# First head's weights as contiguous rows, constants joined to x's first tile, and constant products on TensorE ahead of the first weights

## The chip, the cores and the metric

The kernel runs on one core of a Trainium2 chip. The metric is the device time of one execution in microseconds (us). Before the change it is 1331.93 us, the median of three runs (1330.86, 1331.93 and 1333.83). In the profile, PE is TensorE, PEld its weight loads, DVE is VectorE, ACT is ScalarE, POOL is GpSimd, and SP is the engine that issues most DMAs.

## What is computed

One layer of a streaming encoder on x (512 tokens by 2048 channels, float32), cut to what matters:

```python
hn = rmsnorm(x, norm_g)                       # 512 x 2048
proj = einsum('bsd,dc->bsc', hn, w_in)        # q, k, v, gate of 3 branches; 4 forget logits; merge gates
f_logit = proj[..., QKVG_COLS:QKVG_COLS + N_HEADS] + b_f
gates = sigmoid(proj[..., QKVG_COLS + N_HEADS:] + b_gate)   # 3 x 2048
ya, yb, yc = forgetting(...), chunked(...), stick_breaking(...)   # 4 heads of 128 each
ys = stack([ya, yb, yc]) * silu(gate_paths)
merged = sum(gates * einsum('bsnw,nwd->bsnd', ys, w_up), axis=2)
out = x + merged @ w_out
```

## The kernel before, in words

**Layout.** Everything is held transposed: channels on the 128 partitions, the 512 tokens along the row. x is 16 tiles of 128x512 (kt 0 to 15). Each float32 operand of a product is split into a rounded part (`hi`, type fp32r) and the rest (`lo`), and hi·hi + hi·lo + lo·hi is summed: ScalarE rounds (L243, or L426 for x, where norm_g is multiplied in), VectorE subtracts (L247, or L429 for x). The row norm is not applied to x but to the products afterwards, by the tile `rstd` (L497, used at L505). Most projections use a seven-product scheme over pairs of column blocks (`PairTask`), where some weight sums are made by a DMA that adds on landing (`add_up`, L282, issued by POOL).

**Units.** The work on TensorE is a list of units, each with one tile of weights: a load (`load_unit`, L370, into one of six `raw` tiles), a rounding (`prep`, L384, into one of three `wh`/`wl` pairs), and its products (all at L262). The first nine units (`first_quad`, L1165) are the first head: q, k, v and gate at once, in a sweep over the 16 tiles of x in the order of `spans` (L413): kt 0, then kt 1, then (8, 9), (2, 3), (10, 11) and so on. A unit of one kt has 12 products of 512 columns: four of weight hi with x hi, four of weight hi with x lo, four of weight lo with x hi. A unit of two kts has 24. Between them stand the forget logits (L1213). After the sweep come two gate columns (`gate_units(late=True)`, L1154) and the rest of the heads.

**What orders the work.** A planner (`Flow`, L63) keeps a clock for PE, ACT and DVE, with costs and due times that the tasks name (`due` in `prep_x` L422, `DUE` in `combos` L510, `landing` L267 for DMAs), and writes the order of these three engines out. Each engine then runs its list in order and waits by semaphore. DMAs of SP stand in program order (`fetch`, L275); every eighth reuses a semaphore and waits for the DMA eight before it. The tiles `t2` (21 of them, `NT`) hold x, the loads of `xn` (x again, token by token, for the row norms, L466) and, later, results; one of them is `rstd`.

**The start.** ACT issues the load of the constants `small_in` (L293: norm_g, b_f, b_gate and others, 133 numbers a partition), then that of the first unit's weights. SP issues x kt 0, x kt 1, the second unit's weights, x kt 8, x kt 9, the third unit's weights, and so on. The first head's weights are cut out of the array `w_col` by a four-piece access (`src`, L1240): 128 numbers (512 bytes) a piece for the first two units, 256 (1 KB) for the others. `prep_x` rounds x kt 0 on ACT, then DVE subtracts; `prep` rounds the first weights on ACT, then DVE subtracts.

Of the kernel before, what the change touches and what calls it, by code (L numbers as in the profile page):

```python
# [15 lines left out]
P = 128  # L16
# [46 lines left out]
class Flow:  # L63
# [16 lines left out]
    def give(self, slots, n=1):  # L80
        slots.free += [self.fin] * n
# [80 lines left out]
def hybrid_kernel(  # L162
# [1 line left out]
    tc: tile.TileContext,  # L164
    xT: bass.AP,
    xn: bass.AP,
    consts: bass.AP,
    w_col: bass.AP,
    rel: bass.AP,
    w_up: bass.AP,  # L170
# [26 lines left out]
    def t2(s, dt=F32):  # L197
        return tp.tile([P, S], dt, tag="t2", name=nm(s))
# [19 lines left out]
    def two(ap):  # L218

        return ap.rearrange("p (h s) -> p h s", h=2)  # L220
# [19 lines left out]
    def split(hi, lo, src, n, ev=None, due=(), hi_ev=None):  # L240

        yield (ACT, act_us(n), *due)
        nc.scalar.activation(hi, src, AF.Copy)  # L243
        if hi_ev is not None:
            set_(hi_ev)
        yield (DVE, dve_us(n), *due)
        nc.vector.tensor_sub(lo, src, f(hi))  # L247
        if ev is not None:
            set_(ev)
# [17 lines left out]
    def landing(ready, kb):  # L267

        line[0] = max(line[0], ready) + 0.5
        line[1] = max(line[1], line[0] + 1.0) + kb / (325.0 if line[1] < 60.0 else 370.0)  # L270
        return line[1] + 1.5

    first = []

    def fetch(to, src, ready, kb, queue=nc.sync):  # L275
        i = queue.dma_start(to, src)
# [93 lines left out]
    def load_unit(u):  # L370
        if isinstance(u, Pair):
            if u is u.task.units[0]:
                yield from u.task.load()
            return
        for s in u.srcs:
            yield raws, 1
            t = raw_tile(u.shape)
            to = t
            if len(s.shape) > len(t.shape):
                to = t.rearrange("p (c k) m -> p c k m", c=s.shape[1])  # L380
            u.raw = t
            u.there.t = fetch(to, s, flow.ready, 4 * u.shape[0] * P * P // 1024, nc.scalar if u is units[0] else nc.sync).t

    def prep(u):  # L384
        n = u.shape[0] * P
        u.hi = wp.tile([P] + u.shape, F32R, tag="wh", name=nm("wh"), bufs=LA + 1)
        u.lo = wp.tile([P] + u.shape, F32R, tag="wl", name=nm("wl"), bufs=LA + 1)
        yield u.source_there()
        yield from split(u.hi, u.lo, u.source(), n, u.ready, hi_ev=u.ready_hi)
        u.split_done()  # L390


# [17 lines left out]
    del xps.free[UK:]  # L410


    spans = [(0, 1), (1, 2)] + [(k + h, k + h + 2) for k in range(0, UK, 2) for h in (0, UK)][1:]  # L413
    place = {kt: i for i, kt in enumerate(kt for sp in spans for kt in range(*sp))}


# [2 lines left out]

    def prep_x(kt):  # L420

        due = (5.0 + 2.7 * place[kt],)  # L422
        yield x_in[kt]
        x, g, h, lo = xraw[kt], gn[:, kt:kt + 1], xs[kt].hi, xs[kt].lo
        yield (ACT, act_us(S), *due)
        nc.scalar.activation(h, two(x), AF.Copy, scale=g)  # L426
        set_(raw_hi[kt])
        yield (DVE, dve_us(S), *due)
        nc.vector.scalar_tensor_tensor(lo, two(x), g, f(h), op0=ALU.mult, op1=ALU.subtract)  # L429
        set_(raw_ev[kt])  # L430

        due = (DUE[0] - 16.0 + place[kt],)
        if kt % 2 == 0:
            yield (DVE, 0.5, *due)
            nc.vector.tensor_scalar_mul(x, x, g)
# [28 lines left out]
    n_used = [0]  # L464

    def square_x(i, x):  # L466
        yield n_in[i]
# [7 lines left out]
    def norm_x():  # L475

        m, tmp = small_n[:, 2, :], [small_n[:, i, :] for i in range(3, 6)]
        yield DVE, 0.2
        nc.vector.tensor_reduce(m, ssq, axis=AX.X, op=ALU.add)
        yield from rsqrt(rcol, m, D, tmp, 4)  # L480
        yield DVE, 0.1
        nc.vector.tensor_scalar_mul(rcol_s, rcol, SCALE)
        yield t2s, 1
        dg = t2("dg")
        for b in range(QB):
            yield ACT, 0.3
            nc.scalar.activation(dg[:, blk(b)], identf, AF.Copy, scale=rcol[:, b:b + 1])
        yield Event(flow.fin + 3.0)
        yield atts, 1
        ps = att()  # L490
        yield PE, 0.9
        nc.tensor.matmul(ps, onef, dg, start=True, stop=True)
        give(t2s, 2)
        yield t2s, 1
        yield ACT, act_us(S)
        rstd.append(t2("rstd"))
        nc.scalar.activation(rstd[0], ps, AF.Copy)  # L497
        give(atts)
        set_(rstd_ev)

    def by_norm(c, src=None):

        yield rstd_ev
        yield DVE, dve_us(S)
        nc.vector.tensor_mul(c, c if src is None else src, rstd[0][:c.shape[0], :])  # L505
        n_used[0] += 1
        if n_used[0] == NB * DT + NB * NH + NH + 4 * NH + 1:
            give(t2s)

    def combos(k):  # L510

        due = (DUE[0] + 0.5 * k,)
        late = (DUE[1] + 0.5 * k,)
        yield gained[k]
        yield gained[k + UK]
        yield used_f[k // 2]
        a, b = xraw[k], xraw[k + UK]
        q = dve_us(HS)
        yield (DVE, q, *due)
        nc.vector.tensor_sub(a[:, LH], a[:, LH], a[:, RH])  # L520
# [15 lines left out]
        give(t2s)  # L536
# [627 lines left out]

    def first_quad(head):  # L1165

        c0 = head.n * 4 * NH + head.h
        ps, pools = {}, {Q: accs[1], K: accs[2], V: atts, G: atts}
        def mms(i):
            def go(u):  # L1170
# [66 lines left out]
            return  # L1237
            yield

        def src(k0, k1):  # L1240
            half, k0, k1 = k0 // UK, k0 % UK, (k1 - 1) % UK + 1
            return w_col[c0:c0 + 3 * NH + 1:NH, half, :, k0:k1, :].rearrange("c p k m -> p c k m")
        return [Unit(mms(i), after if sp[1] == KT else None, shape=(4 * (sp[1] - sp[0]), P), srcs=[src(*sp)])
                for i, sp in enumerate(spans)]

    def schedule(head, a, b):
# [243 lines left out]

    def loads():
        def x(kt):
            yield t2s, 1
            xraw[kt] = t2("x")
            x_in[kt].t = fetch(xraw[kt], xT[kt], 0.0, 256).t

        def n(i):
            yield t2s, 1
            t = t2("xn")
            n_in[i].t = fetch(t, xn[i // NQ, i % NQ], 0.0, 256).t  # L1500
            spawn(square_x(i, t), 10.0)

        todo = list(range(NQ * QB))
        for i, sp in enumerate(spans):

# [35 lines left out]
    assert not side, side  # L1541


NT = 21
KEPT = 1
NX = 28
# [48 lines left out]
```

## Time and profile before

| what | us |
|---|---|
| median of three runs | 1331.93 |
| the profiled execution, whole | 1331.46 |
| its span, first to last instruction | 1329.7 |
| PE busy in the span | 1317.4 |
| DVE busy | 1134.5 |
| ACT busy | 806.3 |

A row of the timeline reads: start, duration of the merged instructions, engine, line, operation, out<-in, how many; then in brackets the engine's idle time ahead of it and what ended it. A row of the windows reads: stretch, its length, busy time of PE, PEld, DVE, ACT and POOL with the count of instructions, the granted clock of TensorE, the share of the DMA engines, GB/s. A row of the waits reads: engine and line <- who released it: us in total, times, the longest. A row of the chain reads: start, us, what.

### The profile page before, as it was taken

To read this page: it belongs to the slowest core of one execution; us is meant where nothing else is said; L and a number is where in the kernel's file an instruction comes from. 1 tells how busy PE (TensorE), PEld (TensorE's weight loads), DVE (VectorE), ACT (ScalarE), POOL (GpSimd) and SP (SyncE) were. 2 spreads that over 40 slices of the span, in tenths; PEclk is the share of its full clock that TensorE was granted. 3 is DMA by queue.
4 is the path that set the end of the run, shared out by engine and by line. 5 is a ranking of instruction groups with operands and counts; after the bars stand their busy time and mean duration, and the time that the engine had idled before them with its cause. 6 is when DMAs were issued, how large, how long until landed. Compare 5 with 4: busy or idle time off the path is not lost.

```text
span 1329.7 us, 20204 instructions
## 1 busy us (share of the span) xinstructions
PE 1317.4 (99%) x7490; PEld 1149.0 (86%) x7490; DVE 1134.5 (85%) x1675; ACT 806.3 (61%) x1280; POOL 94.8 (7%) x120
## 2 busy tenths in 40 slices
PE   8999999999999999999999999999999999999998
PEld 5888888888888888888888888888888888888887
DVE  7899888788888889888988979888899877897786
ACT  8777557575566665666556665666557655454443
POOL 0000000010000100000010100001000000000100
PEclk9999999999999999999999999999999999999999
DMA  9876677767776777767777677676768856668883
GB/s 312 230 188 171 187 201 188 199 171 200 195 209 165 205 204 184 212 158 210 202 182 205 163 207 200 188 202 175 198 179 273 276 193 193 186 173 241 238 238 108
DMA packets 93251, 266.24 MB, mean 200 GB/s; under 512 B 10576, under 2 KB 17360, under 8 KB 93152
## 3 DMA queue, kind: packets, MB, share of 16 engines
q1 hardware_dynamic: 73472, 203.79, 45.6%
q0 software_dynamic: 15552, 56.63, 24.9%
q10 hardware_dynamic: 4128, 4.53, 1.0%
q8 instruction: 59, 0.97, 0.3%
q14 instruction: 40, 0.33, 0.1%
HBM read 245.21 MB, written 19.70 MB: 199 GB/s over the span
## 4 chain that ended last, share of the span: by engine, by line
PE 98%; DVE 1%; DMA 0%; issue 0%; ACT 0%; DVEq 0%
PE acc L262 84%; PE att L262 8%; PE att L998 1%; PE att L257 1%; PE att L258 1%; PE att L1111 1%; PE att L1112 1%; PE att L259 1%; PE att L1110 1%; DVE wl L247 0%; PE att L1062 0%; DMA raw<-in_w_col 0%; PE att L1213 0%; PE att L899 0%; PE att L900 0%; DVE m L247 0%
## 5 line engine op out<-in xcount | busy, mean ns | idle before, releaser
L247 DVE TENSOR_TENSOR wl<-raw,wh 128x1024 fp32r<-128x1024 f32 (+2 forms) x419 | 500.7, 1198 | 145.0 <-ACT wh L243 137.7
L243 ACT ACTIVATE wh<-raw 128x1024 fp32r<-128x1024 f32 (+2 forms) x419 | 434.7, 1038 | 149.3 <-PE acc L262 61.9
L262 PE MATMUL acc<-x,wh 128*128 128x512 f32 (+1 forms) x1568 | 399.4, 391 | 6.8 <-ACT wh L243 6.8
L262 PEld LDWEIGHTS acc<-x,wh 128*128 128x128 f32 x1568 | 277.6, 190 | 55.8 <-ACT wh L243 7.2
L262 PE MATMUL acc<-t,wh 128*128 128x512 f32 (+1 forms) x1128 | 283.8, 390 | 0.0
L262 PEld LDWEIGHTS acc<-t,wh 128*128 128x128 f32 x1128 | 198.3, 189 | 32.8
L262 PEld LDWEIGHTS acc<-x,wl 128*128 128x128 f32 x1504 | 207.0, 190 | 18.0 <-DVE wl L247 1.7
L262 PE MATMUL acc<-x,wl 128*128 128x256 f32 (+1 forms) x1504 | 217.0, 285 | 0.6 <-DVE wl L247 0.6
L262 PEld LDWEIGHTS acc<-t,wl 128*128 128x128 f32 x1104 | 151.7, 190 | 11.4
L262 PE MATMUL acc<-t,wl 128*128 128x256 f32 x1104 | 155.5, 283 | 0.0
L282 POOL DMA_DIRECT2D raw<-in_w_col x92 | 79.5, 864 | 926.7 <-DMA raw<-in_w_col 529.7
L262 PE MATMUL acc<-m,wh 128*128 128x512 f32 (+1 forms) x512 | 113.7, 366 | 1.5 <-DVE m L247 1.5
L262 PEld LDWEIGHTS acc<-m,wh 128*128 128x128 f32 x512 | 85.5, 190 | 14.4 <-DVE m L247 1.9
L805 ACT ACTIVATE c<-acc 128x256 f32<-128x256 f32 x51 | 19.5, 383 | 97.2 <-PE acc L262 94.2
L772 ACT ACTIVATE u<-acc 128x512 f32<-128x512 f32 x51 | 30.3, 594 | 79.4 <-PE acc L262 79.4
L751 ACT ACTIVATE u<-acc 128x512 f32<-128x512 f32 x52 | 31.1, 598 | 72.2 <-PE acc L262 69.3
L627 DVE TENSOR_TENSOR raw<-raw,raw 128x1024 f32<-128x1024 f32 x54 | 65.9, 1220 | 0.5
L621 DVE TENSOR_TENSOR raw<-raw,raw 128x1024 f32<-128x1024 f32 x54 | 65.9, 1220 | 0.4
L262 PE MATMUL att<-y,wh 128*128 128x512 f32 x256 | 65.8, 389 | 0.0
L262 PEld LDWEIGHTS acc<-m,wl 128*128 128x128 f32 x448 | 60.6, 191 | 3.8
L262 PE MATMUL acc<-m,wl 128*128 128x256 f32 x448 | 62.5, 282 | 0.0
L262 PEld LDWEIGHTS att<-y,wh 128*128 128x128 f32 x256 | 48.1, 188 | 10.0
(191 smaller groups left out, 1389.8 us busy)
## 6 DMA issues: line engine op xcount, KB each, us to landing
raw<-in_w_col SPq DMA_DIRECT2D x237, 512.0 KB, 4.3
raw<-in_w_col POOLq DMA_DIRECT2D x92, 512.0 KB, 6.5
raw<-in_w_out SPq DMA_DIRECT2D x40, 512.0 KB, 4.0
gl<-c SPq DMA_DIRECT2D x48, 256.0 KB, 3.6
raw<-in_w_up SPq DMA_DIRECT2D x32, 384.0 KB, 3.8
sg<-gl SPq DMA_DIRECT2D x48, 256.0 KB, 5.1
raw<-in_w_out POOLq DMA_DIRECT2D x16, 512.0 KB, 6.1
x<-in_xT SPq DMA_DIRECT2D x16, 256.0 KB, 6.4
```

The costliest lines, as they stand in the source:

```text
L243: nc.scalar.activation(hi, src, AF.Copy)
L247: nc.vector.tensor_sub(lo, src, f(hi))
L257: nc.tensor.matmul(ps, lh, rh, start=start, stop=False, skip_group_check=more)
L258: nc.tensor.matmul(ps, lh, rl, start=False, stop=False, skip_group_check=more)
L259: nc.tensor.matmul(ps, ll, rh, start=False, stop=stop, skip_group_check=more)
L262: nc.tensor.matmul(ps, w, x, start=start, stop=stop, skip_group_check=more)
L282: nc.gpsimd.dma_start(to, src, accum_op=ALU.add)
L621: nc.vector.tensor_add(w[1], w[1], w[5])
L627: nc.vector.tensor_add(w[2], w[2], w[1])
L751: nc.scalar.activation(self.u, ps, AF.Copy)
L772: nc.scalar.activation(self.s, ps, AF.Copy)
L805: nc.scalar.activation(c, ps[:, RH], AF.Copy, scale=-1.0)
```

## The change

- `consts` becomes `begin`: x's kt 0 and the constants in one array of 645 numbers a partition, loaded by one DMA, the first of SP. The tile `x_begin` is kt 0; it is no longer a `t2` tile, and `rstd` is later written over it, so that `NT` goes from 21 to 20. `combos(0)` sets `begin_free` in place of giving the tile back.
- The first head's weights are laid out ahead of time as `w_one` (two arrays of 128x512) and `w_two` (seven of 128x1024), so that a partition's row is 2 KB or 4 KB in one piece. The first of them is the first DMA of ACT.
- The first unit's weights are rounded on ACT in two halves of 128x256; the first half sets `ready_hi`.
- x kt 0 is rounded by VectorE (`tensor_scalar_mul`) and not by ScalarE.
- TensorE multiplies ones (bf16 views of `onef`) 16 times into `first_ps` ahead of everything else. `first_ps` is written anew later by the logits.
- The planner's numbers change: 340 for 325 in `landing`, `due` 2.5 for 5.0, `DUE` 45, 55 for 48, 58, `line` and `flow.fin`.

```diff
+    begin_in = cp.tile([P, begin.shape[1]], F32, name="begin_in")
+    x_begin, small_in = begin_in[:, :S], begin_in[:, S:]
+    first = [tc.keep_in_program_order(nc.sync.dma_start(begin_in, begin))]
-    small_in = cp.tile([P, consts.shape[1]], F32, name="small_in")
-    nc.scalar.dma_start(small_in, consts)
...
+        if u is units[0]:
+            for h in range(2):
+                yield ACT, act_us(n // 2)
+                nc.scalar.activation(u.hi[:, 2 * h:2 * h + 2, :], u.source()[:, 2 * h:2 * h + 2, :], AF.Copy)
+                if h == 0:
+                    set_(u.ready_hi)
+            yield DVE, dve_us(n)
+            nc.vector.tensor_sub(u.lo, u.source(), f(u.hi))
+            set_(u.ready)
...
-        due = (5.0 + 2.7 * place[kt],)
+        due = (2.5 + 2.7 * place[kt],)
...
+        if kt == 0:
+            yield (DVE, 0.5, *due)
+            nc.vector.tensor_scalar_mul(h, two(x), g)
...
-    rstd, rstd_ev = [], Event()
+    rstd, rstd_ev, begin_free = [x_begin], Event(), Event()
...
-        yield t2s, 1
+        yield begin_free
         yield ACT, act_us(S)
-        rstd.append(t2("rstd"))
         nc.scalar.activation(rstd[0], ps, AF.Copy)
...
-            return w_col[c0:c0 + 3 * NH + 1:NH, half, :, k0:k1, :].rearrange("c p k m -> p c k m")
+        srcs = [w_one[i] for i in range(N_ONE)] + [w_two[i] for i in range(len(SPANS) - N_ONE)]
...
+    warm = onef.bitcast(BF16)
+    for _ in range(WARM):
+        nc.tensor.matmul(first_ps[:, :2 * P], warm[:, :P], warm, start=True, stop=True)
-    line[:] = 0.8, 3.0
-    flow.fin = 5.0
+    line[:] = 0.8, 1.9
+    flow.fin = 3.5
...
-NT = 21
+NT = 20
+WARM = 16
-DUE = 48.0, 58.0
+DUE = 45.0, 55.0
```

More of the change, by code (lines that the diff above doesn't have):

```diff
@@ L166, in hybrid_kernel @@
     xn: bass.AP,
-    consts: bass.AP,
+    begin: bass.AP,
+    w_one: bass.AP,
+    w_two: bass.AP,
     w_col: bass.AP,
@@ L269, in landing @@
         line[0] = max(line[0], ready) + 0.5
-        line[1] = max(line[1], line[0] + 1.0) + kb / (325.0 if line[1] < 60.0 else 370.0)
+        line[1] = max(line[1], line[0] + 1.0) + kb / (340.0 if line[1] < 60.0 else 370.0)
         return line[1] + 1.5
-    first = []
     def fetch(to, src, ready, kb, queue=nc.sync):
@@ L377, in load_unit @@
             t = raw_tile(u.shape)
-            to = t
-            if len(s.shape) > len(t.shape):
-                to = t.rearrange("p (c k) m -> p c k m", c=s.shape[1])
             u.raw = t
-            u.there.t = fetch(to, s, flow.ready, 4 * u.shape[0] * P * P // 1024, nc.scalar if u is units[0] else nc.sync).t
+            u.there.t = fetch(t, s, flow.ready, 4 * u.shape[0] * P * P // 1024, nc.scalar if u is units[0] else nc.sync).t
     def prep(u):
@@ L388, in prep @@
         yield u.source_there()
-        yield from split(u.hi, u.lo, u.source(), n, u.ready, hi_ev=u.ready_hi)
+        if u is units[0]:
[7 more added lines that the diff above has]
+            set_(u.ready)
+        else:
+            yield from split(u.hi, u.lo, u.source(), n, u.ready, hi_ev=u.ready_hi)
         u.split_done()
@@ L410, in hybrid_kernel @@
     del xps.free[UK:]
-    spans = [(0, 1), (1, 2)] + [(k + h, k + h + 2) for k in range(0, UK, 2) for h in (0, UK)][1:]
+    spans = SPANS
     place = {kt: i for i, kt in enumerate(kt for sp in spans for kt in range(*sp))}
@@ L420, in prep_x @@
     def prep_x(kt):
-        due = (5.0 + 2.7 * place[kt],)
+        due = (2.5 + 2.7 * place[kt],)
         yield x_in[kt]
         x, g, h, lo = xraw[kt], gn[:, kt:kt + 1], xs[kt].hi, xs[kt].lo
-        yield (ACT, act_us(S), *due)
-        nc.scalar.activation(h, two(x), AF.Copy, scale=g)
+        if kt == 0:
+            yield (DVE, 0.5, *due)
+            nc.vector.tensor_scalar_mul(h, two(x), g)
+        else:
+            yield (ACT, act_us(S), *due)
+            nc.scalar.activation(h, two(x), AF.Copy, scale=g)
         set_(raw_hi[kt])
@@ L463, in hybrid_kernel @@
     squared = [0]
-    n_used = [0]
     def square_x(i, x):
@@ L505, in by_norm @@
         nc.vector.tensor_mul(c, c if src is None else src, rstd[0][:c.shape[0], :])
-        n_used[0] += 1
-        if n_used[0] == NB * DT + NB * NH + NH + 4 * NH + 1:
-            give(t2s)
     def combos(k):
@@ L535, in combos @@
         yield from split(h, lo, a[:, RH], HS, ev, late)
-        give(t2s)
+        if k:
+            give(t2s)
+        else:
+            set_(begin_free)
         if k % 2 == 0:
@@ L1165, in first_quad @@
     def first_quad(head):
-        c0 = head.n * 4 * NH + head.h
         ps, pools = {}, {Q: accs[1], K: accs[2], V: atts, G: atts}
@@ L1238, in after @@
             yield
-        def src(k0, k1):
-            half, k0, k1 = k0 // UK, k0 % UK, (k1 - 1) % UK + 1
-            return w_col[c0:c0 + 3 * NH + 1:NH, half, :, k0:k1, :].rearrange("c p k m -> p c k m")
-        return [Unit(mms(i), after if sp[1] == KT else None, shape=(4 * (sp[1] - sp[0]), P), srcs=[src(*sp)])
+        srcs = [w_one[i] for i in range(N_ONE)] + [w_two[i] for i in range(len(SPANS) - N_ONE)]
+        return [Unit(mms(i), after if sp[1] == KT else None, shape=(4 * (sp[1] - sp[0]), P), srcs=[srcs[i]])
                 for i, sp in enumerate(spans)]
@@ L1492, in x @@
         def x(kt):
+            if kt == 0:
+                xraw[kt], x_in[kt].t = x_begin, landing(0.0, 256)
+                return
             yield t2s, 1
@@ L1541, in hybrid_kernel @@
     assert not side, side
-NT = 21
+NT = 20
 KEPT = 1
+WARM = 16
+SPANS = [(0, 1), (1, 2)] + [(k + h, k + h + 2) for k in range(0, UK, 2) for h in (0, UK)][1:]
+N_ONE = 2
 NX = 28
@@ L1571, with first @@
     rel = g["rel_bias"][0]
+    xT = g["x"][0].T.reshape(DT, P, S)
+    cols = [C * 4 * NH + r * NH for r in range(4)]
+    def first(k0, k1):
+        half, k0, k1 = k0 // UK, k0 % UK, (k1 - 1) % UK + 1
+        return w_col[cols, half, :, k0:k1, :].transpose(1, 0, 2, 3).reshape(P, -1, P)
     at = np.clip(np.arange(P)[:, None] + S - P - np.arange(S)[None, :], -128, 128) + 128
     arrays = {
-        "xT": g["x"][0].T.reshape(DT, P, S),
+        "xT": xT,
         "xn": g["x"][0].reshape(QB, P, DT // NQ, S).transpose(0, 2, 1, 3),
-        "consts": np.concatenate(consts, axis=1),
+        "begin": np.concatenate([xT[0]] + consts, axis=1),
+        "w_one": np.stack([first(*sp) for sp in SPANS[:N_ONE]]),
+        "w_two": np.stack([first(*sp) for sp in SPANS[N_ONE:]]),
         "w_col": w_col,
```

## The prediction

> **What bounds the kernel now.** I read the page first, then the windows, the waits of PE, and the timeline of the first 20 us and of the end of the sweep.
>
> The page, engines and chain:
>
> ```profile
> PE 1317.4 (99%) x7490; PEld 1149.0 (86%) x7490; DVE 1134.5 (85%) x1675; ACT 806.3 (61%) x1280; POOL 94.8 (7%) x120
> PE 98%; DVE 1%; DMA 0%; issue 0%; ACT 0%; DVEq 0%
> ```
>
> TensorE is the bound: 98% of the chain that ended last is its work. The windows, cut where something changes:
>
> ```profile
> 0.00:6.60 6.60, 0.02 (x1) 0.02 (x1) 2.71 (x12) 2.71 (x4) 1.52 (x12) 1.00 0.60 168
> 6.60:11.70 5.10, 5.10 (x12) 4.04 (x13) 3.96 (x6) 3.12 (x5) 0.00 (x0) 1.00 0.95 328
> 11.70:58.50 46.80, 46.80 (x216) 34.49 (x216) 41.36 (x88) 40.86 (x95) 2.74 (x3) 1.00 0.94 304
> 58.50:70.30 11.80, 11.00 (x90) 10.59 (x89) 11.80 (x19) 8.77 (x18) 0.00 (x0) 1.00 0.41 96
> 70.30:1326.00 1255.70, 1254.23 (x7175) 1099.79 (x7176) 1074.23 (x1552) 750.82 (x1161) 90.58 (x105) 1.00 0.71 197
> ```
>
> From 70.30 to 1326.00 PE lacks 1.47 us of being always busy, so the rest of the program follows whatever PE wins or loses before, us for us. Besides that and the last stores, PE idles at two places: 6.6 us at the start, and 0.8 us in 58.5 to 70.3, where VectorE is full (11.80 of 11.80). The waits of PE say the same of the start:
>
> ```profile
> PE acc L262 <- ACT wh L243: 6.8, 2, 6.6
> ```
>
> A second loss shows in no idle time. The chain, in pairs of products:
>
> ```profile
> 6.58 1.22 PE acc L262 x2
> 10.36 0.85 PE acc L262 x2
> 11.97 0.47 PE acc L262 x2
> ```
>
> The first twelve products of 512 columns follow each other every 0.425 us (0.85 for two), the next ones every 0.23. They are the x12 of the window 6.60:11.70. The granted clock column stands at 1.00 in that window, so here the pitch and not that column tells the clock. The slow stretch costs 12 x (0.425 - 0.23) = 2.3 us. So three sums can be won: up to 6.6 us of start, 2.3 us of slow products, 0.8 us later.
>
> **The change, part by part.** The start now:
>
> ```profile
> 0.87 0.20 POOL L306 MEMSET tmpc<- 128x128 f32 x1
> 1.26 0.45 ACTq L276 DMA_DIRECT2D raw<-in_w_col  x1
> 3.99 0.72 ACT L426 ACTIVATE x<-x,small_in 128x512 fp32r<-128x512 f32 x1 [1.90 <-DMA small_in<-in_consts]
> 4.19 0.21 DVE L332 TENSOR_SCALAR gq<-small_in 128x1 f32<-128x1 f32 x2
> 4.74 0.75 DVE L429 SCALAR_TENSOR_TENSOR x<-x,small_in,x 128x512 fp32r<-128x512 f32 x1 [0.34 <-ACT x L426]
> 5.53 0.49 DVE L435 TENSOR_SCALAR x<-x,small_in 128x512 f32<-128x512 f32 x1
> 5.90 0.63 ACT L243 ACTIVATE wh<-raw 128x512 fp32r<-128x512 f32 x1 [1.19 <-DMA raw<-in_w_col]
> 6.56 0.69 DVE L247 TENSOR_TENSOR wl<-raw,wh 128x512 fp32r<-128x512 f32 x1 [0.54 <-ACT wh L243]
> ```
>
> *Weights' arrival.* They are issued at 1.26, behind the constants, and end ACT's wait at 5.90. After the change they are ACT's first DMA (the constants' place, 0.83) and have 128 rows of 2 KB instead of 512 pieces. The windows of the start give the rate:
>
> ```profile
> 1.00:2.00 1.00, 0.00 (x0) 0.00 (x0) 0.62 (x3) 1.00 (x1) 0.89 (x6) 1.00 0.14 35
> 2.00:3.00 1.00, 0.00 (x0) 0.00 (x0) 0.39 (x3) 0.08 (x1) 0.23 (x1) 1.00 0.81 189
> 3.00:4.00 1.00, 0.00 (x0) 0.00 (x0) 0.01 (x1) 0.01 (x1) 0.00 (x0) 1.00 1.04 378
> 4.00:5.00 1.00, 0.00 (x0) 0.00 (x0) 0.66 (x5) 0.71 (x1) 0.00 (x0) 1.00 0.93 249
> 5.00:6.00 1.00, 0.00 (x0) 0.00 (x0) 0.96 (x2) 0.10 (x1) 0.00 (x0) 1.00 0.64 141
> 6.00:7.00 1.00, 0.42 (x1) 0.42 (x2) 0.46 (x2) 1.00 (x2) 0.00 (x0) 1.00 0.69 209
> 7.00:8.00 1.00, 1.00 (x3) 0.74 (x3) 0.93 (x2) 0.34 (x2) 0.00 (x0) 1.00 0.94 349
> ```
>
> By 4.0 us 602 KB have come; `begin` (330 KB) and the first weights (262 KB) are 592 KB. Some of x kt 1, queued behind `begin` on SP, is mixed in, so I take 4.45 us for the weights, between 4.0 and the 5.9 of today. `begin` (today's x kt 0 and constants, usable at 3.99) I take at 4.0.
>
> *Rounding.* Only half the weights are rounded before the first product: 0.40 us by the nearest row of that size,
>
> ```profile
> 27.20 0.40 ACT L243 ACTIVATE x<-x 128x256 fp32r<-128x256 f32 x1
> ```
>
> in place of 0.63, so 4.45 + 0.05 + 0.40 = 4.9, and 0.05 to the product (6.53 to 6.58 today): 4.95. x kt 0 goes to VectorE at about 4.2 (two small copies first) and takes 0.49 as L435 does: 4.7, in time. Then x lo (0.75) ends at 5.65, L435 at 6.1, weight lo (0.69) at 6.8; the products that need them come 4 and 8 products later, at 5.9 and 6.8 even at the fast pitch. ACT loses one rounding of x (0.72), which VectorE takes over at 0.49; VectorE was idle then. Nothing of this reaches PE.
>
> *The constants.* `onef` is written by 1.07; 16 products of 256 columns follow. Their slow pitch is not in the trace: below the 0.425 of 512 columns, above half of it (0.21). Fast, sixteen of 256 columns take 2.08,
>
> ```profile
> 61.37 2.08 PE L262 MATMUL acc<-x,wh 128*128 128x256 f32 x16
> ```
>
> 0.13 each against 0.23, so I take the same part of 0.425, 0.24: 3.9 us, ending at 5.0 (bounds 4.5 and 7.9). So the first real product starts at 5.0 instead of 6.58: **1.6 us**.
>
> *The clock.* Today the pitch turns fast 5.1 us after the first product. From 1.1 us the same gives 6.2, so products between 5.0 and 6.2 are still slow: a loss of 1.2 x (1 - 0.23/0.425) = 0.55 us instead of 2.3, **1.75 us** won. Bounds: nothing lost (2.3 won), or the constants do not count and all 2.3 are lost again. The Trainium skill (TensorE: Matmul & The Clock Gate, Part 1: The HAM clock gate) says that the clock is raised after a busy window of about 3.4 us, and that these windows run freely and do not start with the kernel; the trace's 5.1 us, more than one window and less than two, agrees. By that rule an estimate for the turn here is anywhere from 4.5 to 7.9, with a gain from 1.0 to 2.3 in place of the 1.75; rival 1 prices the late end from rows.
>
> *The third unit.* 1.6 + 1.75 = 3.35 us earlier PE asks for the third unit's weights, which are late enough today to be the next wait:
>
> ```profile
> 12.34 1.06 ACT L243 ACTIVATE wh<-raw 128x1024 fp32r<-128x1024 f32 x1 [1.90 <-DMA raw<-in_w_col]
> 14.57 0.61 PE L262 MATMUL acc<-x,wh 128*128 128x512 f32 x2
> ```
>
> PE will want them at 14.57 - 3.35 = 11.2, so they must land by 10.1. From 4 to 8 us only 948 KB moved (249, 141, 209, 349), in the stretch where the 512-byte pieces are under way. At 375 they take 2.5 us: landing at 12.34 - 1.5 = 10.8 at the latest reckoning. With the whole rest (2.16 MB up to this unit, less 602 KB) at 375 after 4.0 and 0.4 for the signal it is 8.6. The middle, 9.7, costs nothing; 10.8 costs 0.7. From the fourth unit on the weights are rounded long before PE wants them:
>
> ```profile
> 16.99 1.04 ACT L243 ACTIVATE wh<-raw 128x1024 fp32r<-128x1024 f32 x1
> 21.24 0.62 PE L262 MATMUL acc<-x,wh 128*128 128x512 f32 x2
> 38.40 1.06 ACT L243 ACTIVATE wh<-raw 128x1024 fp32r<-128x1024 f32 x1 [0.67 <-PE att L262]
> ```
>
> Rounded at 18.03, wanted at 21.24; at 38.40 ACT itself waits for PE to give back a `wh`. So ACT, and behind it the `xn` loads on SP and the weights that follow them in SP's queue, move with PE.
>
> *The end of the sweep.* Here a planner's list decides, and the changed order differs:
>
> ```profile
> 49.40 1.27 ACT L487 ACTIVATE dg<-identf,small_n 128x128 f32<-128x128 f32 x4
> 54.84 1.02 PE L492 MATMUL att<-dg,tmpc 128*128 128x512 f32 x2
> 56.33 2.01 ACT L243 ACTIVATE wh<-raw 128x1024 fp32r<-128x1024 f32 x2 [1.66 <-DMA raw<-in_w_col]
> 57.42 2.36 DVE L247 TENSOR_TENSOR wl<-raw,wh 128x1024 fp32r<-128x1024 f32 x2 [1.96 <-ACT wh L243]
> 59.70 0.69 DVE L505 TENSOR_TENSOR f<-att,rstd 128x512 f32<-128x512 f32 x1
> 68.98 2.35 DVE L247 TENSOR_TENSOR wl<-raw,wh 128x1024 fp32r<-128x1024 f32 x2
> 70.26 1.22 PE L262 MATMUL acc<-x,wl 128*128 128x256 f32 x8 [0.62 <-DVE wl L247]
> ```
>
> ACT waits until 56.33 for the adding DMA's sum; from 57.42 to 70.2 VectorE works without a break and PE waits 0.62 for it (0.18 before, for ACT). After the change the norm's product (L492) stands eight products earlier, `rstd` and the product f stand ahead of the wait, in the 1.96 us that VectorE idles, and the combination c1 (0.41) behind the late `wl`. So VectorE's run from the sum to that `wl` is 0.69 + 0.41 = 1.1 us shorter, and the 0.8 us can go. Against that: ACT has one more `xn` square and one split less ahead of its 38.40 (0.4 us), so the sum may gain some 0.4 us less than PE. I take **0.4 us**, bounds 0 and 0.8. L492 stays unhurried: `dg` is done at 50.67 today, four us ahead of it, and eight products are 1.8.
>
> *Costed at nothing.* The reuse of x kt 0's tile for `rstd`, with `NT` 20: as many `t2` tiles are free for `xn` as before (21 - 1 - 16 = 20 - 1 - 15). POOL's list is the same, SP's and ACT's differ in single swaps after the first rows. PE's order after the sweep is the same instruction for instruction.
>
> **The sum.** 1.6 + 1.75 + 0.4 = 3.75 us, against the profiled execution's 1331.46: 1327.7. That execution lies 0.5 us below the median of the runs (1331.93), so for the median I say **1328.1**.
>
> **The rivals.**
> 1. *The clock turns late, or the first weights come late.* If the constants count for half, because their columns are few or because PE pauses behind them, the turn comes halfway between 6.2 and 10.1 (5.1 us after the first real product), at 8.1: a loss of 1.4 in place of 0.55. Then the third unit waits for nothing and the gain is 1.6 + 0.9 + 0 to 0.4, 1329.0 to 1329.4. If the first weights land at 5.4 and not 4.45, another 1.0 goes: 1330.4. For it: the constants last 3.9 us, less than the 5.1 that the turn takes today. Against: by 4.0 us the DMAs have moved enough for `begin` and these weights.
> 2. *The change does not do what it says*: constants do not raise the clock at all. Then the gain is 1.6 + 0.4, 1329.9, within the first rival's times.
> 3. *The sum at the first gate column does not move.* If POOL's adding DMA still lands at 56.3, VectorE's run ends 1.1 us earlier at best, and 3.35 us won become an idle PE at 69: the gain is 1.1, 1330.8. The same place gives the slow side: the kernel gets slower from the point where that DMA lands more than 1.1 us later than now, at 57.4; crowded behind loads that now come in a burst it could land at 60, 2.6 us past the point: 1334.5. Against: its source is queued behind `xn` loads that move with PE.
> 4. *All of it goes well*: 1.6 + 2.3 + 0.8 = 4.7, 1327.2; with weights at 4.0 and constants at 4.5, 1326.7.
>
> **How the numbers follow.** Forecast with its own spread (1327.3 to 1329.2) 0.55; rivals 1 (0.17) and 2 (0.05) together 0.22; rival 3 0.08 without loss and 0.06 as a loss; rival 4 0.09. The range leaves out the loss and the ends of the rest: 1326.2 to 1331.2. About 0.2% (2.7 us) is what a measurement of this kernel can tell from no change; that is 1329.3. Faster by more: the forecast, rival 4 and a little of the first: 0.66. Slower by more: most of rival 3's loss, 0.05. Within: 0.29.
>
> **What would show it.** Right: the first product with `wh` at 5.0; the pitch 0.23 from about 6; the third unit's products at 11.2 without idle time; no idle PE between 55 and 67; the rest the same. Wrong: products at 0.425 beyond 8 us; ACT waiting for `raw` of the third unit past 10.1; PE idle behind `wl` at the first gate column.

## The result, and the profile after

The changed kernel takes 1328.58 us (median of five runs, 1326.86 to 1329.00) against 1332.21 for the kernel before beside it (five runs, 1330.86 to 1333.83). The ratio is 0.9964, 95% interval 0.9953 to 0.9975: faster by 0.36%. The profiled execution went from 1331.46 to 1328.65, so by 2.81 us, and its span from 1329.7 to 1326.9. By the medians the gain is 3.63 us; the profiled execution of before lay 0.75 under its median. The changed kernel's five runs stand in two groups, 1326.9 and 1327.0 against 1328.6 to 1329.0; the experiments come back to that.

The page's engines and the waits of PE after the change:

```profile
PE 1320.2 (99%) x7506; PEld 1150.5 (87%) x7506; DVE 1134.7 (86%) x1676; ACT 805.9 (61%) x1280; POOL 94.9 (7%) x120
```

```profile
PE acc L264 <- DVE m L249: 1.5, 2, 1.3
PE att L1544 <- POOL tmpc L307: 1.1, 1, 1.1
PE acc L264 <- DVE gq L333: 0.7, 1, 0.7
```

PE is as full as before. The 6.6 us of waiting at the start have become 1.1 ahead of the constants and 0.7 behind them. The first row, 1.5 us near 1183, is the same in both kernels. The waits at the first gate column are gone.

The timeline of the start (start, us, engine, line, operation; idle time and releaser in brackets), and then the chain (start, us, what):

```profile
0.83 0.39 ACTq L276 DMA_DIRECT2D raw<-in_w_one  x1
...
1.13 3.60 PE L1544 MATMUL att<-tmpc 128*128 128x256 bf16 x16 [1.13 <-POOL tmpc L307]
...
4.61 0.17 DVE L331 COPY gq<-begin_in 128x4 f32<-128x4 f32 x1 [2.04 <-DMA begin_in<-in_begin]
...
4.79 0.72 ACT L390 ACTIVATE wh<-raw 128x256 fp32r<-128x256 f32 x2 [2.71 <-DMA raw<-in_w_one]
4.79 0.48 DVE L435 TENSOR_SCALAR x<-begin_in 128x512 fp32r<-128x512 f32 x1
...
5.42 1.19 PE L264 MATMUL acc<-x,wh 128*128 128x512 f32 x2 [0.69 <-DVE gq L333]
```

```profile
5.42 1.19 PE acc L264 x2
...
9.17 0.85 PE acc L264 x2
10.02 0.48 PE att L264 x2
10.51 0.46 PE acc L264 x2
```

The constants run from 1.13 to 4.73, 0.225 us each. `begin` ends VectorE's wait at 4.61, the weights end ScalarE's at 4.79, and the first product starts at 5.42. In the chain two products still take 0.85 us at 9.17, and about 0.47 from 10 on: in this execution the clock turns near 10, sixteen constants or not.

The loads, by the windows of the start (stretch, length, busy time of PE, PEld, DVE, ACT, POOL, granted clock, DMA share, GB/s):

```profile
4.00:5.00 1.00, 0.72 (x4) 0.18 (x2) 0.39 (x3) 0.21 (x1) 0.00 (x0) 1.00 1.11 396
5.00:6.00 1.00, 0.58 (x2) 0.52 (x3) 1.00 (x4) 1.00 (x3) 0.00 (x0) 1.00 1.00 383
6.00:7.00 1.00, 1.00 (x4) 0.81 (x3) 0.96 (x3) 0.23 (x1) 0.00 (x0) 1.00 1.07 412
7.00:8.00 1.00, 1.00 (x4) 0.81 (x3) 1.00 (x3) 0.95 (x2) 0.00 (x0) 1.00 1.02 418
```

Where the pieces of 512 bytes and 1 KB moved 141 to 349 GB/s, whole rows move 383 to 418. The third unit's weights are rounded with no wait ahead of them, and its products follow the second unit's without a gap, in the timeline:

```profile
9.66 1.06 ACT L245 ACTIVATE wh<-raw 128x1024 fp32r<-128x1024 f32 x1
```

```profile
13.09 0.62 PE L264 MATMUL acc<-x,wh 128*128 128x512 f32 x2
```

The end of the sweep, in the timeline:

```profile
52.60 0.60 ACT L507 ACTIVATE begin_in<-att 128x512 f32<-128x512 f32 x1
...
53.41 0.68 DVE L515 TENSOR_TENSOR f<-att,begin_in 128x512 f32<-128x512 f32 x1
53.78 2.01 ACT L245 ACTIVATE wh<-raw 128x1024 fp32r<-128x1024 f32 x2 [0.58 <-DMA raw<-in_w_col]
...
67.54 1.12 PE L264 MATMUL acc<-x,wl 128*128 128x256 f32 x8
68.50 1.72 PE L264 MATMUL acc<-t,wh 128*128 128x256 f32 x13
```

`rstd` is done and f is begun ahead of the adding DMA's sum, which lands at 53.78 in place of 56.33. The product behind `wl` at 67.54 has no idle time. The next row, the first product of `t`, ends the stretch. In the kernel before it stands here:

```profile
71.31 1.96 PE L262 MATMUL acc<-t,wh 128*128 128x256 f32 x15
```

PE's gate columns begin at 58.46 before and at 56.99 after, in the two timelines:

```profile
58.46 2.11 PE L262 MATMUL acc<-x,wh 128*128 128x256 f32 x16
```

```profile
56.99 2.08 PE L264 MATMUL acc<-x,wh 128*128 128x256 f32 x16
```

So this stretch took 12.85 us and now takes 11.51, which is four times the 2.88 that 24 products need. From that product on, the last product follows 1254.70 us later in both. So the 2.81 us are 1.47 won up to the end of the sweep and 1.34 won in the 12 us behind it, where the idle column had shown only 0.8.

### The profile page after: what moved, and what is told of

It reads as the page before. It is cut to its first block, busy times and chain, and to the rows that moved or that the text cites. A ratio compares the mean times of both kernels' runs of the same rounds, so it can differ in the third digit from the quotient of the medians.

```text
span 1326.9 us, 20238 instructions
## 1 busy us (share of the span) xinstructions
PE 1320.2 (99%) x7506; PEld 1150.5 (87%) x7506; DVE 1134.7 (86%) x1676; ACT 805.9 (61%) x1280; POOL 94.9 (7%) x120
## 4 chain that ended last, share of the span: by engine, by line
PE 98%; DVE 1%; DMA 0%; issue 0%; DVEq 0%
PE acc L264 84%; PE att L264 8%; PE att L1008 1%; PE att L259 1%; PE att L260 1%; PE att L1121 1%; PE att L1122 1%; PE att L261 1%; PE att L1120 1%; PE att L1072 0%; PE att L1222 0%; DMA begin_in<-in_begin 0%; PE att L909 0%; PE att L910 0%; DVE m L249 0%; DVE wl L249 0%
```

## Experiments

**Theories.** In the kernel before, three things could have cost these 2.8 us and more in the faster runs: the late start, the slow clock, and the wait at the first gate column. For the last there were two readings: the order of the planner's list there (norm ahead of the sum), or the moment at which the adding DMA's sum lands.

One table holds what the profiles say. S is where PE could begin the gate columns (the start of the first product there, less the idle time ahead of it); "landed" is the start of ACT's split of the adding DMA's sum; "ahead" is S less landed; "lost" is the time from S to the first product of `t`, less 11.51.

| execution | us | first product | clock turns | S | landed | ahead | lost |
|---|---|---|---|---|---|---|---|
| before | 1331.46 | 6.58 | 11.72 | 58.46 | 56.33 | 2.13 | 1.34 |
| after | 1328.65 | 5.42 | 9.93 | 56.99 | 53.78 | 3.21 | 0.00 |
| e1, no constants | 1329.32 | 5.80 | 10.89 | 57.64 | 53.75 | 3.89 | 0.00 |
| e2, 20 constants | 1326.75 | 5.61 | 3.82 | 55.12 | 52.06 | 3.06 | 0.00 |
| e3, norm's times alone | 1334.68 | 6.66 | 11.08 | 58.80 | 58.67 | 0.13 | 4.31 |
| e4, rows alone | 1329.08 | 5.90 | 9.84 | 57.19 | 54.02 | 3.17 | 0.30 |
| e5, old numbers | 1331.37 | 5.38 | 9.32 | 56.82 | 54.71 | 2.11 | 1.36 |
| e6, x ahead | 1326.79 | 5.39 | 4.55 | 55.14 | 52.28 | 2.86 | 0.01 |
| e7, constants alone | 1333.63 | 6.69 | 4.27 | 57.50 | 57.09 | 0.41 | 3.07 |
| e8, x by ACT | 1328.73 | 5.91 | 9.56 | 57.08 | 53.65 | 3.43 | 0.00 |
| e9, changed again | 1326.88 | 5.77 | 4.90 | 55.23 | 51.98 | 3.25 | 0.00 |
| e10, x ahead again | 1326.76 | 5.32 | 4.93 | 55.12 | 52.04 | 3.08 | 0.01 |
| e11, old norm times | 1328.66 | 5.67 | 9.68 | 57.00 | 53.35 | 3.65 | 0.00 |
| e12, old start numbers | 1332.90 | 5.60 | 10.31 | 57.41 | 56.48 | 0.93 | 2.35 |

The turns are the trace's records of the clock; the pitch of the products (0.425, then 0.23) changes at the same place. In e1 the split did not wait for the sum, so there 53.75 is the latest that it can have landed. In e3 the 4.31 hold a stretch at half the clock (see there).

### e1: no constants (changed kernel)

```diff
-WARM = 16
+WARM = 0
```

> The changed kernel without the 16 constant products; the rest of the lists is the same. Theory A (of the prediction: the constants start the count for the clock): without them the pitch turns fast 5.1 us after the first real product, and the time is 1.0 to 1.8 us above the changed kernel's, about 1330.0. Theory B (the pause of 0.7 us between the last constant and the first real product voids them, except when the turn happens to fall well): the time stays within 0.6 us of the changed kernel's 1328.6, and the turn comes 3.4 to 6.8 us after the first real product in either.

Measured: 1328.94 (11 runs, 1328.19 to 1330.68), ratio 0.9981, 0.9972 to 0.9989. Without a single constant half of the gain or more is still there (0.19% against the changed kernel's 0.36% by the ratios), and nothing is lost at the gate column. The clock turns 5.1 us after the first product, as in the kernel before. The time is theory B's and not theory A's. None of its runs is in the group at 1326.9.

### e2: twenty constants (changed kernel)

```diff
-WARM = 16
+WARM = 20
```

> 20 constant products instead of 16: at 0.225 us each they end at 5.6 in place of 4.7, so TensorE doesn't pause ahead of the first real product, which starts 0.2 us later. Theory A: no gain, within 0.3 us of the changed kernel. Theory B: the stretch from 1.1 us on is then busy throughout, the pitch turns fast between 4.5 and 8 us, and the time falls by about 1.5 us to 1327 (0.5 at least).

Measured: 1328.23 (seven runs, 1326.68 to 1328.72), ratio 0.9968, 0.9957 to 0.9978. In its profile the constants turn the clock by themselves, at 3.82, and end at 4.78, so that PE pauses 0.83 us all the same. That execution takes 1326.75: the faster group is the one with the early turn. The median is 0.35 us under the changed kernel's 1328.58: theory A allowed 0.3, theory B asked for 0.5 at least, so it decides neither.

### e3: the norm's due times alone (kernel before)

```diff
-DUE = 48.0, 58.0
+DUE = 45.0, 55.0
```

> The kernel before with DUE = 45, 55 alone. In the lists this puts rstd and f ahead of the first gate column's rounded weights on ACT and DVE; the start is as before. Theory C (the order of the lists removes the waits at the first gate column): PE idles at most 0.3 us between 58 and 70, and the time falls by 0.8 to 1.3 us, to about 1331.0. Rival D (those waits went because PE and the adding DMA stand otherwise to each other after the faster start): no change, 1332.2.

Measured: 1334.19 (11 runs, 1332.31 to 1336.26), ratio 1.0015, 1.0006 to 1.0024: slower. So an earlier norm is no gain by itself. The list of ACT moved with it, the sum landed at 58.67 in place of 56.33, and PE stood still for it. Neither theory had that. The timeline, then the windows of what follows (the third number from the end is the granted clock):

```profile
60.73 2.57 PE L262 MATMUL acc<-x,wh 128*128 128x256 f32 x16 [1.93 <-ACT wh L243]
```

```profile
58.80:62.28 3.48, 1.55 (x13) 1.55 (x14) 2.52 (x3) 3.48 (x7) 0.58 (x1) 1.00 0.92 152
62.28:65.69 3.41, 3.41 (x19) 3.41 (x18) 3.41 (x7) 2.19 (x5) 0.00 (x0) 0.50 0.42 70
```

The pause of 1.93 us was followed by 3.41 us at half the clock, where PE is full but its products of 256 columns follow each other every 0.213 us in place of 0.12.

### e4: whole rows alone (kernel before)

```diff
...
-            return w_col[c0:c0 + 3 * NH + 1:NH, half, :, k0:k1, :].rearrange("c p k m -> p c k m")
...
+        srcs = [w_one[i] for i in range(N_ONE)] + [w_two[i] for i in range(len(SPANS) - N_ONE)]
...
```

> The kernel before with w_one and w_two alone: whole rows, the constants still in a load of their own and ahead of the first weights on ACT's queue, the three lists as before. By the prediction's step on the weights: they land at about 5.0 instead of 5.9, the third unit's at 10 instead of 12.3; the first product starts at about 5.6, and the time falls by 0.9 us to 1331.3. Rival: the constants' load in front, and not the 512-byte pieces, is what holds the weights; then the first product stays at 6.3 or later and the time within 0.3 us.

Measured: 1330.92 (11 runs, 1329.08 to 1332.93), ratio 0.9990, 0.9982 to 0.9999. The profiled execution is the fastest of these. In it the sum lands 3.17 us ahead instead of 2.13, and 0.30 are lost instead of 1.34, with the old list. So the loads alone can bring most of the gain at the gate column. The first product comes at 5.90, between the 5.6 expected and the rival's 6.3. In the four windows from 4 to 8 us the DMAs moved 373, 262, 371 and 406 GB/s, against 249, 141, 209 and 349 before, so the whole rows themselves made the loads faster. Part of this execution's lead is chance: its clock turned 3.9 us after the first product, 5.1 before. What x's first tile and the constants in one load are worth alone was not run.

### e5: all four planner numbers old (changed kernel)

```diff
-        line[1] = max(line[1], line[0] + 1.0) + kb / (340.0 if line[1] < 60.0 else 370.0)
+        line[1] = max(line[1], line[0] + 1.0) + kb / (325.0 if line[1] < 60.0 else 370.0)
...
-        due = (2.5 + 2.7 * place[kt],)
+        due = (5.0 + 2.7 * place[kt],)
...
-    line[:] = 0.8, 1.9
-    flow.fin = 3.5
+    line[:] = 0.8, 3.0
+    flow.fin = 5.0
...
-DUE = 45.0, 55.0
+DUE = 48.0, 58.0
```

> The changed kernel with the four numbers of the planner as they were (rate 325, first x due at 5.0, line from 3.0 and 5.0, norm due at 48 and 58), so mostly the old list at the first gate column, with the new loads and constants. Theory L (the adding DMA's landing decides there, and whole rows have brought it forward): it still lands some 3 us ahead of the end of the sweep, at most 0.3 us are lost from the sweep's end to the first product of the next unit on top of its 11.5, and the time is that of the changed kernel, 1328.3 to 1329.2. Theory O (the new order of the list is what filled the gap, as the prediction had it): 0.8 to 1.3 us are lost there again, 1329.5 to 1330.0.

Measured: 1330.90 (11 runs, 1328.30 to 1332.62), ratio 0.9984, 0.9975 to 0.9993. The time is above what either theory said. 1.36 us are lost at the gate column, as theory O had it, but by the means that theory L named: the sum lands only 2.11 ahead. The rest of the excess over the changed kernel's 1328.65 is 1.5 us near 1187 (under e12).

### e6 and e10: x's first tile ahead of the small copies, twenty constants (changed kernel)

```diff
-    nc.vector.tensor_copy(gq, gqk)
...
+        if kt == 0:
+            small_copies()
...
-WARM = 16
+WARM = 20
```

> The changed kernel with 20 constants, and x's first tile rounded ahead of the small copies on VectorE. Theory S (after the change these two copies and x's rounding hold the first product, not the weights): the first product comes with the weights' first half, at 5.1 to 5.3 in place of 5.42 and 5.61, unless the constants themselves run slowly to 5.65; time 1327.6 to 1328.2, so 0.2 to 0.4 under the run with 20 constants. Theory W (the weights' landing holds it): first product at 5.4 or later and the time as with 20 constants, 1328.2 or more.

> 20 constants and x's first tile ahead of the small copies, beside the changed kernel on one chip. Theory G: the constants run into the first product with at most 0.25 us between them, so some window that begins after 1.1 us is full and the turn comes by 8.0 us at the latest: every run between 1326.6 and 1328.3, the median 0.5 to 1.8 under that of the changed kernel. The rival, that the low median of its first five runs was chance: the same median as the changed kernel within 0.3.

Measured: 1326.79 (five runs, 1326.65 to 1328.19) and then 1328.44 (five runs, 1326.76 to 1328.73), ratios 0.9960 (0.9948 to 0.9973) and 0.9966 (0.9953 to 0.9978). The first product comes at 5.39 and 5.32, PE now waiting for the weights:

```profile
5.39 0.73 PE L264 MATMUL acc<-x,wh 128*128 128x512 f32 x2 [0.25 <-ACT wh L392]
```

That lies between what the two theories of e6 asked for (5.3 at most, 5.4 at least). So the copies held it by little; the weights' rounding ends nearly as late. The first low median was chance: the ten runs of this version and the ten of the changed kernel (e9 counted in) have the same mean, 1327.6, and no version here beats the changed kernel. Theory G's claim for e10, every run below 1328.3, failed in three of five; its rival's, the same median as the changed kernel beside it, failed too (1326.88 there).

### e7: constants alone (kernel before)

```diff
+    warm = onef.bitcast(BF16)
+    for _ in range(WARM):
+        nc.tensor.matmul(first_ps[:, :2 * P], warm[:, :P], warm, start=True, stop=True)
...
+WARM = 24
```

> The kernel before with 24 constants ahead of the first product, and nothing else of the change: they run from 1.1 to 6.5, where PE had been idle. Theory L (what PE wins ahead of the loads is given back where it waits for them): the first twelve products run at 0.23 or part of them do, PE then waits for the third unit's weights (rounded at 12.3 to 13.4 as before), so at most 1.7 of the 2.3 us are won there, and at the first gate column the adding DMA, which hasn't moved, takes most of that back: 1331.5 to 1332.4, and 1.3 us lost at the gate column before become 2 to 3. Theory K (the clock is a gain of its own): 1330.1 to 1330.9.

Measured: 1332.05 (11 runs, 1330.40 to 1333.63), ratio 0.9997, 0.9989 to 1.0006: no difference, as theory L said. There are 24 constants here, as the wait is longer. The timeline of the profiled execution, the slowest of these, shows where the gain went:

```profile
6.69 0.73 PE L262 MATMUL acc<-x,wh 128*128 128x512 f32 x2 [1.26 <-ACT wh L243]
...
11.36 0.61 PE L262 MATMUL acc<-x,wl 128*128 128x512 f32 x2
11.81 0.61 PE L262 MATMUL att<-x,wl 128*128 128x512 f32 x2
13.27 0.74 PE L262 MATMUL acc<-x,wh 128*128 128x512 f32 x2 [0.84 <-ACT wh L243]
...
59.15 2.18 PE L262 MATMUL acc<-x,wh 128*128 128x256 f32 x16 [1.65 <-ACT wh L243]
```

The products run at 0.23 from the first on, then PE waits 0.84 for the third unit's weights and 1.65 at the gate column, because the loads have not moved forward (landed 57.09).

### e8: x's first tile rounded by ACT (changed kernel)

```diff
-        if kt == 0:
-            yield (DVE, 0.5, *due)
-            nc.vector.tensor_scalar_mul(h, two(x), g)
-        else:
-            yield (ACT, act_us(S), *due)
-            nc.scalar.activation(h, two(x), AF.Copy, scale=g)
+        yield (ACT, act_us(S), *due)
+        nc.scalar.activation(h, two(x), AF.Copy, scale=g)
```

> The changed kernel with x's first tile rounded by ACT, as before the change (0.72 us ahead of the weights' first half, 0.40, on the same engine). Theory S: both then stand in line on ACT behind begin's landing at 4.6: first product at 5.8 to 5.9 in place of 5.42, the time 0.3 to 0.5 longer, 1328.9 to 1329.1. If PE's start is not what sets the end by then (theory L at its strongest, the loads give the pace everywhere), no difference: 1328.6.

Measured: 1328.67 (seven runs, 1326.75 to 1329.17), ratio 0.9969, 0.9958 to 0.9980. The first product comes at 5.91, as expected. But S is 0.09 us later than in the changed kernel, not 0.5: the clock turned at 9.56 there, so the later start only meant fewer slow products. In time no difference can be seen.

### e9: the changed kernel again

No edit.

> The changed kernel once more, beside the next three on one chip. Theory G (the clock is raised in windows of 3.41 us whose place is chance, and the pause of 0.69 us between the constants and the first product spoils a window): its runs fall into two groups, 1326.6 to 1327.2 where the turn comes early and 1328.2 to 1329.0 where it comes near 10 us, more of them late than early: median 1328.0 to 1328.7. If a start of 5.42 and a turn near 10 belong to every execution: one group at 1328.6.

Measured: 1326.88 (five runs: 1326.59, 1326.61, 1326.88, 1326.97, 1328.63), ratio 0.9959, 0.9946 to 0.9971. Two groups again, but four of five are early; "more of them late" was not borne out. Its profile is the early kind:

```profile
1.13 3.59 PE L1544 MATMUL att<-tmpc 128*128 128x256 bf16 x16 [1.13 <-POOL tmpc L307]
5.77 0.70 PE L264 MATMUL acc<-x,wh 128*128 128x512 f32 x2 [1.05 <-DVE gq L333]
6.31 0.62 PE L264 MATMUL att<-x,wh 128*128 128x512 f32 x2
...
11.34 0.62 PE L264 MATMUL acc<-x,wh 128*128 128x512 f32 x2
```

The very same instructions start 0.35 us later than in the first profile, and the third unit begins at 11.34 against 13.09, because the clock turned at 4.90 and no real product was slow.

### e11 and e12: which of the four numbers

e11 takes back the norm's due times, e12 the other three:

```diff
-DUE = 45.0, 55.0
+DUE = 48.0, 58.0
```

```diff
-        line[1] = max(line[1], line[0] + 1.0) + kb / (340.0 if line[1] < 60.0 else 370.0)
+        line[1] = max(line[1], line[0] + 1.0) + kb / (325.0 if line[1] < 60.0 else 370.0)
...
-        due = (2.5 + 2.7 * place[kt],)
+        due = (5.0 + 2.7 * place[kt],)
...
-    line[:] = 0.8, 1.9
-    flow.fin = 3.5
+    line[:] = 0.8, 3.0
+    flow.fin = 5.0
```

> The changed kernel with the norm's due times alone as they were (48 and 58). Theory N (of the four old numbers these made the loss at the first gate column, by more squares of xn behind the split that waits for PE): the adding DMA lands within 2.5 us of the sweep's end instead of 3.2 ahead of it, 0.8 to 1.3 us are lost there, 1329.5 to 1330.5. Theory M (the start's numbers do it, through ACT's order): lands 3 us or more ahead, nothing lost, 1328.0 to 1328.9.

> The changed kernel with the other three numbers as they were (325, first x due at 5.0, line from 3.0 and 5.0), and the norm's due times new (45 and 55). Theory N: as the changed kernel, 1328.0 to 1328.9, landing some 3 us ahead. Theory M: 0.8 to 1.3 us lost at the gate column, 1329.5 to 1330.5.

Measured: e11 1328.58 (seven runs, 1328.03 to 1329.27), ratio 0.9971, 0.9960 to 0.9983; e12 1330.47 (11 runs, 1329.51 to 1332.90), ratio 0.9990, 0.9981 to 0.9999. Theory N falls, theory M holds: the three numbers of the start, not told apart here, make the loss. (The 2.35 of the table is from e12's slowest run; the median is within theory M's range.) The queue of SP shows how, in the timeline of the changed kernel and then of e12:

```profile
38.92 0.33 SPq L276 DMA_DIRECT2D xn<-in_xn  x1
39.34 3.47 SPq L276 DMA_DIRECT2D raw<-in_w_col  x6
```

```profile
39.18 1.55 SPq L276 DMA_DIRECT2D xn<-in_xn  x3
40.83 4.36 SPq L276 DMA_DIRECT2D raw<-in_w_col  x6
```

ACT squares the `xn` tiles, and behind its split that waits for PE (36.92, 37.18 in e12) stand five squares in the changed kernel, six before, seven in e12. The last `xn` loads wait for tiles that these squares give back, and the gate column's weights queue behind them. With three `xn` bunched ahead, the first of these weights took 6.26 us from issue to landing in e12 (40.83 to 47.09), 4.18 in the changed kernel (39.34 to 43.52), 6.00 before (41.13 to 47.13). POOL's adding DMA follows that landing by 0.6 us. All fourteen profiles go with this: in the eight with one `xn` load issued behind ACT's last split of the sweep the first of these weights took 3.6 to 4.2 us to land, in the six with two or three (before, e3, e4, e5, e7, e12) 4.7 to 6.3.

The profiled execution of e12, its slowest run, also shows the 1.5 us near 1187. Its windows, and those of the kernel before:

```profile
1184.00:1187.90 3.90, 2.43 (x16) 1.93 (x14) 3.90 (x11) 1.06 (x1) 0.00 (x0) 1.00 0.88 181
1187.90:1191.30 3.40, 3.40 (x14) 3.11 (x14) 3.40 (x6) 0.68 (x1) 0.31 (x1) 0.50 0.75 211
1191.30:1195.00 3.70, 3.70 (x21) 3.19 (x20) 2.15 (x3) 1.75 (x3) 0.55 (x1) 1.00 0.70 105
```

```profile
1185.90:1189.30 3.40, 2.10 (x16) 1.89 (x15) 3.40 (x6) 0.00 (x0) 0.00 (x0) 1.00 0.95 219
1189.30:1193.00 3.70, 3.70 (x22) 3.19 (x21) 3.70 (x6) 1.29 (x2) 0.86 (x1) 1.00 0.55 129
```

Both kernels pause near 1185 for VectorE (the 1.5 us of the waits). In e12 and e7 both parts of the pause (0.16 and 1.31) fell into one window of the clock, in e5 the longer part and the end of the other (1.37), and the next window ran at 0.50; in the profile of before 1.30 idle fell into one window, and the clock stayed. From the first product of `t` to the last of all e5, e7 and e12 take 1256.2 us, all others 1254.7. That this makes part of the scatter of the timed runs is argued from four profiles, not shown for each run.

## Why the prediction was right, point by point

The time forecast (1328.1, range 1326.2 to 1331.2) holds; the terms of its sum do not, one by one, so that it holds is in part luck. Both groups of runs (1326.9 and 1328.6) lie in the range.

- **What bounds the kernel.** Right. PE is the bound, and behind the gate column the program follows us for us: 1254.70 us in both.
- **Weights' arrival, 4.45, and `begin`, 4.0.** Measured 4.79 and 4.61. The first lies within its bounds; `begin` had none and came 0.6 late. So x's rounding, which was to be in time at 4.7, ended at 5.27, after the weights' first half (0.40 from 4.79, about 5.2), and the first product came at 5.42, in other profiles of the same start at 5.38 to 5.77, in place of 5.0. The start was worth 0.8 to 1.2 us in place of 1.6.
- **The constants, 0.24 each, ending at 5.0.** Right: 0.225, 4.73.
- **The clock, 1.75.** This is the step that failed as a single number. From the first to the 13th product the kernel before takes 5.22 us (6.58 to 11.80), the changed kernel 4.92 (5.42 to 10.34) in one profile and 2.85 (5.77 to 8.62) in the other. So in these two the clock gave 0.30 or 2.37, never the 1.75 in between; 6.2 as a turn was seen in no profile. The first lies between rival 1 (turn at 8.1, 0.9 won) and rival 2 (nothing won), with its turn at 9.93; the second is the "all 2.3 won" of the bounds. Of the ten turns with constants in front three lie in the other estimate there, 4.5 to 7.9. Nor is 5.1 a fixed wait: without constants the clock turned 5.1, 5.1, 4.4 and 3.9 us after the first product (before, e1, e3, e4).
- **The third unit.** Right: `raw` was there by 9.66 (9.7 forecast), and no product waited, nor in e9, where PE came to them at 11.34 (11.2 forecast). e7 shows the price without whole rows: 0.84.
- **The end of the sweep, 0.4.** The place was right; the size was not (1.34), and the way was so only in part. Two reasons for the size. The loss was read from the idle column (0.8), but a late `wl` also shows as a longer pitch; the stretch against its bare 11.51 says 1.34. And the sum was taken to gain 0.4 us less than PE; it gained 2.55 (56.33 to 53.78) where PE gained 1.47. The one square more ahead of ACT's split was counted as a delay of that split, and not as one less behind it, where the loads hang on it. So most of the 1.34 came by what the prediction had working against it: at the fixed 3.47 of the next point, 1.08 is the landing's longer lead (2.13 to 3.21), and 0.26 is left for the order of the norm. e3 has that order without the landing, and lost; e11 has the landing with the old due times, and lost nothing.
- **The price of being late there.** The table gives it: in the four profiles with the norm's product f behind the split and a loss (before, e4, e5, e7) ahead and lost add up to 3.47 or 3.48 us each time. VectorE's run from the sum to that `wl` is a fixed length. In e6, with f ahead of the split, 2.86 ahead costs nothing (0.01), so the run is at least 0.6 shorter; in e12, with f ahead too but other work behind it, the two add up to 3.28, 0.2 shorter. The prediction had it 1.1 shorter.
- **Rival 3** named the place and the sign of the danger. Not the adding DMA's standing still, but its moving more than PE, is what happened; e3, e7 and e12 are what it would have cost.

In the profiled pair 1.16 + 0.30 + 1.34 = 2.80 of the 2.81 us, where the sum had 3.75. By luck the gate column gave back 0.94 of the 1.89 that the start (0.44) and the clock (1.45) lacked.

## What to carry to other kernels

A gain at the start of a kernel is kept only as far as the loads behind it move too: constants on TensorE alone gave nothing here (0.9997), whole rows alone 0.10% (e4), all of the change but the constants 0.19% (e1), and the whole 0.36%. Where an engine's run has a fixed length from a landing to the product that needs it, compare that length with how far the landing is ahead, and read the loss from the pitch against the bare time, not from the idle column. If TensorE's clock has to be raised, expect the time in groups and profile more than one execution before a term is judged.

## What the runs showed of the hardware that was not expected

- **The turn of the clock is a matter of place as well as of work.** With constants from 1.13 on, the clock turned at 3.82, 4.27, 4.55, 4.90 and 4.93 in five profiles and at 9.32, 9.56, 9.68, 9.93 and 10.31 in five others, and nowhere between. The records are whole steps of 3.41 us (1317.55 and 1320.96 us of full clock). Counted back in such steps, the windows ahead of the early turns begin between 0.41 and 1.52, those that did not turn the clock between 2.49 and 3.48, so that they hold the 0.65 to 1.18 us between the constants and the first product. The Trainium skill (TensorE: Matmul & The Clock Gate, Part 1: The HAM clock gate) says that windows of about 3.4 us run freely and do not begin with the kernel; the traces agree. Whether it is the pause that makes a turn late stays open: e6 and e10, with 0.25 and no pause, turned early in their profiles, but four of e10's five runs are in the slower group. Nor does PE's busy share alone decide. In the windows of e2, then e5, then the changed kernel (first profile), about equally busy (2.69, 2.77 and 2.72 us), the first raised the clock at its end and the other two did not:

```profile
0.41:3.82 3.41, 2.69 (x13) 1.96 (x14) 1.01 (x5) 1.28 (x1) 1.42 (x11) 1.00 0.55 127
```

```profile
2.49:5.91 3.42, 2.77 (x12) 1.76 (x11) 1.43 (x7) 1.12 (x3) 0.00 (x0) 1.00 0.95 357
```

```profile
3.10:6.51 3.41, 2.72 (x11) 1.76 (x10) 1.86 (x8) 1.44 (x3) 0.00 (x0) 1.00 1.04 388
```

- **A pause far shorter than a window lowers the clock.** 1.47 us without a product in one window (e7, e12) and 1.87 of the 1.93 (e3) were each followed by 3.41 us at 0.50; 1.30 us in one window (before) were not. The same section of that page has the clock fall after an idle window of about 3.4 us; these traces differ, and 1.47 us in a window was enough. The border is not sharp in these rows: with PE busy 2.04 us, e5's window was followed by 0.50, and e1's was not (e5, then e1).

```profile
1183.51:1186.92 3.41, 2.04 (x12) 1.73 (x13) 3.41 (x9) 0.56 (x1) 0.00 (x0) 1.00 0.90 196
1186.92:1190.33 3.41, 3.41 (x13) 2.93 (x12) 3.41 (x5) 1.06 (x1) 0.86 (x1) 0.50 0.41 126
```

```profile
1181.66:1185.08 3.42, 2.04 (x14) 1.57 (x12) 3.42 (x9) 1.06 (x1) 0.00 (x0) 1.00 0.95 184
1185.08:1188.49 3.41, 3.32 (x20) 2.98 (x21) 3.41 (x7) 0.00 (x0) 0.00 (x0) 1.00 0.92 246
```

- **The granted clock's column reads 1.00 in stretches where products of 512 columns take 0.425 us** (before 10 us in the first profile of the changed kernel). There the pitch tells the clock.
